# A hybrid decoder layer on one core: a third PSUM bank for the input projection, taken from the depthwise convolution's running sum

## The chip, the core and the metric

The kernel runs on one core of a Trainium2 chip. Five engines work side by side, each through its own queue in order: TensorE (PE in the profile, its weight loads PEld), VectorE (DVE), ScalarE (ACT), GpSimd (POOL) and SyncE (SP), which only issues transfers; ScalarE issues some too. They wait for each other by semaphores. SBUF is the working memory, PSUM holds matmul results in banks of 128 x 512 fp32 values. The metric is the device time of one launch in microseconds; less is better.

## What is computed

One layer over 2048 tokens of width 1024, all in fp32. A normalized input is projected once to 3080 columns, which feed three mixers; their outputs are joined, projected and added, and a SwiGLU feed-forward of inner width 2816 follows.

```python
h = rms_norm(x, norm1_g[l])
u = jnp.einsum('btd,de->bte', h, w_in[l])
u_conv, u_qkv, u_z, u_ab, u_dq, u_dk, u_dv = jnp.split(u, [...], axis=-1)
y_conv = conformer_conv_mixer(u_conv, ...)      # gate, 31-tap depthwise conv, layer norm, silu
y_gdn = gated_deltanet_mixer(u_qkv, u_z, u_ab, ...)   # chunks of 64, triangular solve, scan
y_diff = differential_attention_mixer(u_dq, u_dk, u_dv, ...)  # causal, two softmaxes per head
y = jnp.concatenate([y_conv, y_gdn, y_diff], axis=-1)
x = x + jnp.einsum('bte,ed->btd', y, w_out[l])
h = rms_norm(x, norm2_g[l])
gate, up = jnp.split(jnp.einsum('btd,df->btf', h, w_ffn_in[l]), 2, axis=-1)
x = x + jnp.einsum('btf,fd->btd', jax.nn.silu(gate) * up, w_ffn_out[l])
return rms_norm(x, final_norm_g)
```

The convolution: for each of 256 channels and each token, the sum over 31 earlier values of `val * sigmoid(gate)` times a weight, plus a bias.

## The kernel before

Tokens are worked in four units of 512 (`U`). Every large product is done three times in a two-part format: weights and activations are split into a high and a low part, and `mm3` (lines 136 to 139) adds high x high, high x low and low x high into one bank. A weight piece comes from memory as `wr`; ScalarE writes its high part (line 120) and GpSimd the low part as a difference (line 121), in two halves each, into one of three buffers `wp`. For the input projection the split pieces are also written to memory (`ws`, line 124), so units 1 to 3 load them without a split. Thus the splits of the input projection, and their GpSimd work, lie in unit 0 alone.

The steps of the first part are named in the string at line 937, two characters each, kind and unit: I is the projection to `mz` (gate columns) and `mq` (six tiles of q, k, v for the delta net, each with a 4-tap convolution, lines 321 to 336), C the projection to `mg` and `mv` and the 31-tap convolution, K the attention's q and k (`ma`, eight tiles), V its values (`mw`), N the input norm (`ht`), L the layer norm after the convolution, and G the delta net: products `kk`, the solve of 62 short VectorE operations in series (lines 466 to 472, `tm` and `Tt`, ended by the copy to `Lg` at line 473), a way through memory (`gT`, back to `X64`), the products `yp` and `wp`, and a scan over chunks (`vp`, `op`, `dp`). A0 is the attention of unit 0 (`s` scores, `pt` transposes, `po` output).

A projection tile takes its bank from `mmt` in turn (line 181: two banks, `mm0` and `mm1`). It is free when ScalarE and VectorE have taken the result out: for `ma` and `mw` ScalarE writes the high part (`qh`, `ve`), then VectorE the low part (`ql` at lines 708 and 711, `ve` at 728), and both go to memory from two buffers.

The convolution (`conv_taps`, lines 583 to 594) runs on VectorE. Per unit and per tile of 128 channels it does 31 operations of 512 columns: the first multiplies and adds the bias (line 591), thirty multiply and add (line 593). The sum stands in one PSUM bank `cp` (pool `ps_ca`, line 190), and the last operation writes it to SBUF, `ca`. As there is one bank, the second channel tile begins when the first is done.

At A0 the pool context `p1bctx` closes (line 955) and its four banks become those of the attention (`b0`, lines 956 to 958): scores, transposes, and outputs.

The order within each engine's queue is not written by hand. A scheduler with its own time estimates places every instruction; `hp(n)` raises the priority of what is inside it. So a change of pools or operations moves instructions on all engines, also where the diff touches nothing. After the first part, attention of units 1 to 3 is interleaved with the output projection and feed-forward of earlier units.

Of the kernel before, what the change touches and what calls it, by code (L numbers as in the profile page):

```python
# [10 lines left out]
F32 = mybir.dt.float32  # L11
F32R = mybir.dt.float32r
AF = mybir.ActivationFunctionType
ALU = mybir.AluOpType
AX = mybir.AxisListType
PSUM = bass.MemoryType.PSUM
DRAM = bass.MemoryType.DRAM

P = 128
# [3 lines left out]
U = 512  # L23
# [24 lines left out]
def body(ctx: ExitStack, tc: tile.TileContext, x, norm1_g, w_in, conv_dw_w, conv_dw_b,  # L48
# [3 lines left out]
    V, G, A, T = nc.vector, nc.gpsimd, nc.scalar, nc.tensor  # L52
# [20 lines left out]
    def cst(shape, name):  # L73
        return const.tile(shape, F32, name=name, tag=name)
# [26 lines left out]
    def hp(n=4000):  # L101
        return tc.high_priority(offset=n)
# [54 lines left out]
    def slots(pool, tag, n):  # L157
        return [(pool, f"{tag}{i}") for i in range(n)]

    def bank(*b):  # L160
        return Rot([P, 512], F32, *b)
# [19 lines left out]
    mmt = bank(*slots(ps_mm, "mm", 2))  # L181
# [5 lines left out]
    p1bctx = ExitStack()  # L187
    ps_tp = p1bctx.enter_context(tc.tile_pool(name="ps_tp", bufs=2, space=PSUM))
    ps_ga = p1bctx.enter_context(tc.tile_pool(name="ps_ga", bufs=1, space=PSUM))
    ps_ca = p1bctx.enter_context(tc.tile_pool(name="ps_ca", bufs=1, space=PSUM))  # L190


    x0 = [p1b.tile([P, D], F32, name=f"x1_0_{tt}", tag=f"x1{tt}") for tt in range(2)]
# [20 lines left out]
    cwT = cst([P, 2, 34], "cwT")  # L214
# [368 lines left out]
    def conv_taps(u, hc):  # L583

        acc2 = gd.tile([P, 2, U], F32, name=f"ca{u}", tag="ca")
        for ct in range(2):
            acc = ps_ca.tile([P, U], F32, name=f"cp{u}_{ct}", tag="cp")
            for j in range(31):
                w, hj = cwT[:, ct, j:j + 1], hc[:, ct, j:j + U]
                if j == 0:  # L590
                    V.tensor_scalar(acc, hj, w, cwT[:, ct, 31:32], op0=ALU.mult, op1=ALU.add)
                else:
                    V.scalar_tensor_tensor(acc2[:, ct, :] if j == 30 else acc, hj, w, acc, op0=ALU.mult, op1=ALU.add)  # L593
        return acc2

    def conv_ln(u, acc2):
# [81 lines left out]
    def conv_in(u):  # L678

        hts = HT[u]  # L680
        hc = gd.tile([P, 2, 30 + U], F32, name=f"hc{u}", tag="hc")
        G.tensor_copy(hc[:, :, 0:30], hist30)
        for ct in range(2):
            pg = mmt(f"mg{u}_{ct}")
            x_tile8(pg, hts, w_col_piece(w_in, COL_CONV + 256 + ct * P))
            tg_ = hc[:, ct, 30:30 + U]
            with hp():
                A.activation(tg_, pg, AF.Tanh, scale=0.5)
            pv = mmt(f"mv{u}_{ct}")
            x_tile8(pv, hts, w_col_piece(w_in, COL_CONV + ct * P))  # L690
            with hp():
                V.scalar_tensor_tensor(hc[:, ct, 30:30 + U], tg_, 1.0, pv, op0=ALU.add, op1=ALU.mult)
        G.tensor_copy(hist30, hc[:, :, U:U + 30])
        return hc
# [229 lines left out]
    def cut(t, n, m):  # L924

        return [t[:, i * n:(i + 1) * n] for i in range(m)]
# [10 lines left out]
    for step in ("I0 C0 G0 V0 N1 K0 L0 I1 G1 N2 C1 L1 K1 V1 I2 G2 C2 N3 K2 I3 G3 L2 C3 V2 A0 K3 V3 L3").split():  # L937
        what, u = step[0], int(step[1])
        if what == "N":
            HT[u] = ln1(u)  # L940
        elif what == "I":
            gdn_in(u)
        elif what == "G":
            with hp(GP):
                gdn_unit(u, QT[u], SC[u])
        elif what == "K":
            attn_qk(u)
        elif what == "V":
            attn_v(u)
        elif what == "C":  # L950
            CV[u] = conv_taps(u, conv_in(u))
        elif what == "L":
            conv_ln(u, CV[u])
        else:
            p1bctx.close()
            ps0 = ctx.enter_context(tc.tile_pool(name="ps0", bufs=1, space=PSUM, reuse_waits="tile"))
            b0 = slots(ps0, "b0", 4)
            sct, ptt, tot, pot = (bank(b) for b in b0)
            E0, W0 = (p1b.tile([P, 4096], F32, name=f"arena{g}", tag=f"ht{g}") for g in range(2))
            X0, X1 = (p1b.tile([P, D], F32, name=f"arenx{g}", tag=f"x1{g}") for g in range(2))  # L960
            Ep, Wp = cut(E0, 1024, 4), cut(W0, 1024, 4)
            Eq = [e[:, 512:1024] for e in Ep]
            AT.update(e0=Views(F32, *(e[:, 0:512] for e in Ep)), dm=Views(F32, Eq[0]), ob=Views(F32, *cut(Eq[1], 256, 2)),
                      e1=Views(F32, *Eq[2:4]), on=Views(F32, *(f3(c_) for c_ in cut(X0[:, 0:512], 256, 2))),
                      vv=Views(F32R, f4(Wp[0])), kk=Views(F32R, *cut(Wp[1], 512, 2)), pp=Views(F32R, f3(Wp[2])),
                      qq=Views(F32R, *(f3(c_) for c_ in cut(Wp[3], 512, 2) + cut(X1, 512, 2))))
            so_ = [0]

            def take(w, m):
                o = so_[0]  # L970
                so_[0] += w * m
                vs_ = cut(X0[:, 512 + o:], w, m)
                return Views(F32, *([v.rearrange("p (a b) -> p a b", a=2) for v in vs_] if w == 4 else vs_))
            AT.update(small(take))
            dm = dists(U)
            run(attn_unit(0))
# [287 lines left out]
```

## Time and profile before

| what | value |
|---|---|
| median of 3 runs | 2919.01 us (2917.42 to 2922.89) |
| profiled execution | 2917.14 us |
| its span | 2915.4 us |
| TensorE busy | 2800.1 us, 96% |
| VectorE busy | 1565.9 us, 54% |
| ScalarE busy | 1050.0 us, 36% |
| GpSimd busy | 1111.3 us, 38% |
| mean granted TensorE clock | 0.982 |

Durations come from the profiled execution. Shares over the whole span mix stages with different limits, so the tables by stretch count for more. Of a wait the trace names the instruction that came last. Names in the trace leave out the numbers of buffers: `ql` stands for all such tiles. [...]

### The profile page before, as it was taken

The numbers are of one execution on the slowest core, as the hardware profiler recorded it, in microseconds if no ns is written. First come the engines' busy times: TensorE is split into PE (matmuls) and PEld (weight loads), VectorE is DVE, ScalarE is ACT, GpSimd is POOL, SyncE is SP. The second block draws the span as 40 slices with busy tenths as digits, with TensorE's granted clock in tenths as the row PEclk, the third lists the DMA queues.
The fourth block names the chain that finished last, engine by engine and source line by source line (L and its number), as shares of the span: only waits on it lengthen the run. The fifth ranks groups of instructions, "written<-read, shape, count | busy, mean of one in ns | idle before, by whom it ended". The sixth has DMA issues, their size and how long they took to land.

```text
span 2915.4 us, 39754 instructions
## 1 busy us (share of the span) xinstructions
PE 2800.1 (96%) x14673; PEld 2284.4 (78%) x14673; DVE 1565.9 (54%) x3443; ACT 1050.0 (36%) x2237; POOL 1111.3 (38%) x1021
## 2 busy tenths in 40 slices
PE   7979989999988999999998999999999999999998
PEld 6867777778776788887877888887878888888886
DVE  8976776877766765565566655541332222422223
ACT  4333223322154544444455434442332222322222
POOL 4421010001033444344455434444644444444543
PEclk9989999999988999999999999999999999999999
DMA  7784573654776544444366344324343333323332
GB/s 253 242 274 153 178 232 127 207 179 138 254 200 219 144 131 122 112 126 118 108 182 203 86 130 120 93 88 151 102 149 99 96 94 101 116 87 102 101 94 87
DMA packets 404064, 422.52 MB, mean 145 GB/s; under 512 B 46448, under 2 KB 326170, under 8 KB 392606
## 3 DMA queue, kind: packets, MB, share of 16 engines
q1 hardware_dynamic: 344222, 373.31, 41.8%
q10 hardware_dynamic: 59648, 46.67, 5.1%
q8 instruction: 116, 1.90, 0.3%
q14 instruction: 78, 0.64, 0.1%
HBM read 344.35 MB, written 75.56 MB: 144 GB/s over the span
## 4 chain that ended last, share of the span: by engine, by line
PE 80%; DVE 8%; DMA 6%; issue 2%; ACT 2%; POOL 1%; ACTq 0%; SPq 0%; POOLq 0%; DVEq 0%
PE pg L137 6%; PE pg L138 6%; PE pg L139 6%; PE pu L139 5%; PE pu L137 5%; PE pu L138 5%; PE pd L137 5%; PE pd L138 5%; PE pd L139 5%; PE s L784 3%; PE pt L830 2%; PE po L137 1%; PE po L138 1%; PE po L139 1%; PE ma L137 1%
## 5 line engine op out<-in xcount | busy, mean ns | idle before, releaser
L121 POOL TENSOR_TENSOR wp<-wr,wp 128x512 fp32r<-128x512 f32 (+1 forms) x666 | 906.7, 1386 | 865.4 <-ACT wp L120 847.9
L120 ACT CAST wp<-wr 128x512 fp32r<-128x512 f32 (+1 forms) x666 | 378.6, 617 | 871.5 <-PE pd L139 229.1
L137 PE MATMUL pd<-wp,ac 128*128 128x512 f32 x704 | 279.8, 400 | 9.2 <-DVE x L1154 7.6
L1154 DVE TENSOR_TENSOR x<-x,pd 128x512 f32<-128x512 f32 x192 | 130.4, 685 | 285.6 <-PE pd L139 285.2
L137 PE MATMUL pg<-h,wp 128*128 128x512 f32 x704 | 279.6, 397 | 3.4 <-ACT h L1075 1.7
L138 PE MATMUL pd<-wp,ac 128*128 128x512 f32 x704 | 277.1, 394 | 2.1 <-POOL wp L121 2.1
L139 PE MATMUL pd<-wp,ac 128*128 128x512 f32 x704 | 277.5, 394 | 1.5 <-DVE ac L1138 1.5
L139 PE MATMUL pu<-h,wp 128*128 128x512 f32 x704 | 278.4, 396 | 0.0
L139 PE MATMUL pg<-h,wp 128*128 128x512 f32 x704 | 278.3, 395 | 0.0
L137 PE MATMUL pu<-h,wp 128*128 128x512 f32 x704 | 277.3, 394 | 0.6 <-DVE ft L1135 0.6
L138 PE MATMUL pu<-h,wp 128*128 128x512 f32 x704 | 277.8, 395 | 0.0
L138 PE MATMUL pg<-h,wp 128*128 128x512 f32 x704 | 277.6, 394 | 0.0
L1134 DVE SCALAR_TENSOR_TENSOR ft<-ft,pg 128x512 f32<-128x512 f32 x88 | 60.4, 686 | 244.1 <-ACT ft L1133 244.1
L784 PE MATMUL s<-kk,qq 128*128 128x512 f32 (+3 forms) x576 | 171.6, 384 | 5.5 <-DVE mx L787 5.1
L593 DVE SCALAR_TENSOR_TENSOR cp<-hc,cwT,cp 128x512 f32<-128x512 f32 x232 | 173.2, 747 | 2.5
L137 PEld LDWEIGHTS pd<-wp,ac 128*128 128x128 f32 x704 | 132.7, 188 | 45.8 <-DVE x L1154 15.1
L137 PEld LDWEIGHTS pg<-h,wp 128*128 128x128 f32 x704 | 132.3, 188 | 36.2 <-ACT wp L120 5.4
L139 PEld LDWEIGHTS pd<-wp,ac 128*128 128x128 f32 x704 | 132.5, 188 | 31.7 <-DVE ac L1138 3.1
L138 PEld LDWEIGHTS pd<-wp,ac 128*128 128x128 f32 x704 | 132.8, 189 | 30.2 <-POOL wp L121 3.5
L137 PEld LDWEIGHTS pu<-h,wp 128*128 128x128 f32 x704 | 132.3, 188 | 30.0 <-ACT wp L120 1.0
L138 PEld LDWEIGHTS pu<-h,wp 128*128 128x128 f32 x704 | 132.3, 188 | 29.7
L138 PEld LDWEIGHTS pg<-h,wp 128*128 128x128 f32 x704 | 132.3, 188 | 28.8 <-DVE h L1076 0.2
(389 smaller groups left out, 5866.0 us busy)
## 6 DMA issues: line engine op xcount, KB each, us to landing
wr<-in_w_ffn_in_dram SPq DMA_DIRECT2D x176, 512.0 KB, 3.9
wp<-ws SPq DMA_DIRECT2D x66, 1024.0 KB, 5.8
wr<-in_w_ffn_out_dram SPq DMA_DIRECT2D x88, 512.0 KB, 3.5
ws<-wp SPq DMA_DIRECT2D x22, 1024.0 KB, 6.9
wr<-in_w_out_dram SPq DMA_DIRECT2D x44, 512.0 KB, 3.6
arena<-vs SPq DMA_DIRECT2D x80, 256.0 KB, 3.8
kk<-ks SPq DMA_DIRECT2D x64, 256.0 KB, 5.0
qq<-qs SPq DMA_DIRECT2D x96, 128.0 KB, 4.5
```

The costliest lines, as they stand in the source:

```text
L120: A.copy(w[:, 0, q], raw[:, q])
L121: G.tensor_tensor(w[:, 1, q], raw[:, q], w[:, 0, q].bitcast(F32), op=ALU.subtract)
L137: T.matmul(ps, lhsT=lh, rhs=rh, start=start, stop=False)
L138: T.matmul(ps, lhsT=lh, rhs=rl, start=False, stop=False)
L139: T.matmul(ps, lhsT=ll, rhs=rh, start=False, stop=stop)
L593: V.scalar_tensor_tensor(acc2[:, ct, :] if j == 30 else acc, hj, w, acc, op0=ALU.mult, op1=ALU.add)
L784: T.matmul(sp[:, 0:w], lhsT=qq[c][:, l, q0:q0 + P], rhs=kt_[x][c][:, k0:k0 + w], start=l == 0, stop=l == 1)
L830: T.transpose(pt[:, col:col + P], ptile[b][kt // 8][:, (kt % 8) * P:(kt % 8 + 1) * P], ident)
L1134: V.scalar_tensor_tensor(t_, t_, 1.0, pg, op0=ALU.add, op1=ALU.mult)
L1154: V.tensor_tensor(xs_, xs_, pd, op=ALU.add)
```

## The change

The convolution's sum moves from the PSUM bank `cp` to the SBUF tile `ca`, where its result was written anyway; all 31 operations of a channel tile now read and write there. The bank goes to a pool `ps_m3`, which is added to the rotation of `mmt` as a third bank up to A0. There it is taken out again, as the attention uses all four banks.

```diff
     ps_tp = p1bctx.enter_context(tc.tile_pool(name="ps_tp", bufs=2, space=PSUM))
     ps_ga = p1bctx.enter_context(tc.tile_pool(name="ps_ga", bufs=1, space=PSUM))
-    ps_ca = p1bctx.enter_context(tc.tile_pool(name="ps_ca", bufs=1, space=PSUM))
+    ps_m3 = p1bctx.enter_context(tc.tile_pool(name="ps_m3", bufs=1, space=PSUM))
+    mmt.add((ps_m3, "mm2"))
...
         for ct in range(2):
-            acc = ps_ca.tile([P, U], F32, name=f"cp{u}_{ct}", tag="cp")
+            a = acc2[:, ct, :]
             for j in range(31):
                 w, hj = cwT[:, ct, j:j + 1], hc[:, ct, j:j + U]
                 if j == 0:
-                    V.tensor_scalar(acc, hj, w, cwT[:, ct, 31:32], op0=ALU.mult, op1=ALU.add)
+                    V.tensor_scalar(a, hj, w, cwT[:, ct, 31:32], op0=ALU.mult, op1=ALU.add)
                 else:
-                    V.scalar_tensor_tensor(acc2[:, ct, :] if j == 30 else acc, hj, w, acc, op0=ALU.mult, op1=ALU.add)
+                    V.scalar_tensor_tensor(a, hj, w, a, op0=ALU.mult, op1=ALU.add)
...
             p1bctx.close()
+            mmt.slots.pop()
```

Every engine has the same instructions as before, apart from the operands of the taps. Their order changes. In the changed kernel the lines stand one further down from line 190 on.

VectorE, where the solve of unit 0 begins, before. `cp0_1` is the sum of the second channel tile, `ql0_1544_0` the low part of the first q tile, `tm0_0` and `Tt0` the first step of the solve, `ht1` the activations of unit 1.

```order
L593 SCALAR_TENSOR_TENSOR cp0_1_1026<-hc0_850,cwT_126,cp0_1_1026 128x512 x2
L711 SCALAR_TENSOR_TENSOR ql0_1544_0_2086<-ma0_1544_0_2051,qh0_1544_0_2085 128x512
L593 SCALAR_TENSOR_TENSOR cp0_1_1026<-hc0_850,cwT_126,cp0_1_1026 128x512
L470 TENSOR_TENSOR tm0_0_1157<-Lg0_1151,Tt0_1152 64x31
L303 SCALAR_TENSOR_TENSOR ht1_1_1914<-ntp1_1_1_1970,g1T_118,ht1_1_1914 128x128
L303 SCALAR_TENSOR_TENSOR ht1_0_1913<-ntp1_2_0_1991,g1T_118,ht1_0_1913 128x128
```

The same place in the changed kernel; `ca0` is the sum of both channel tiles.

```order
L594 SCALAR_TENSOR_TENSOR ca0_993<-hc0_850,cwT_126,ca0_993 128x512
L304 SCALAR_TENSOR_TENSOR ht1_1_1912<-ntp1_1_1_1968,g1T_118,ht1_1_1912 128x128
L712 SCALAR_TENSOR_TENSOR ql0_1544_1_2124<-ma0_1544_1_2089,qh0_1544_1_2123 128x512
L304 SCALAR_TENSOR_TENSOR ht1_0_1911<-ntp1_1_0_1955,g1T_118,ht1_0_1911 128x128
L304 SCALAR_TENSOR_TENSOR ht1_1_1912<-ntp1_1_1_1968,g1T_118,ht1_1_1912 128x128 x2
L471 TENSOR_TENSOR tm0_0_1155<-Lg0_1149,Tt0_1150 64x31
L473 TENSOR_TENSOR Tt0_1150<-Tt0_1150,tm0_0_1155 64x31
L471 TENSOR_TENSOR tm0_1_1158<-Lg0_1149,Tt0_1150 64x60
```

All 62 taps of unit 0 now stand ahead of the solve (47 of them ahead of the last `kk` eviction); before it was 50 ahead of the solve (35 ahead of that eviction) and 12 between its steps.

TensorE, where the first products of the delta net's unit 0 (`yp0`) stand, before. `mz1_0` and `mz1_1` are tiles of unit 1's projection, `ctq` and `ctp` transposes of the layer norm.

```order
L139 MATMUL mz1_0_2454<-wp26_2449,ht1_1_1914 128x264
L616 MATMUL ctq0_1_2400<-ident_74,cxn0_1_2398 128x128
L604 MATMUL ctp0_2_2405<-ident_74,ca0_993 128x128 x2
L490 MATMUL yp0_1260<-X64_157,L0_477 32x32 x16
L137 MATMUL mz1_1_2484<-wp25_2447,ht1_0_1913 128x264
```

And in the changed kernel.

```order
L138 MATMUL mz1_0_2452<-wp26_2447,ht1_1_1912 128x264
L491 MATMUL yp0_1258<-X64_157,L0_477 32x32 x32
L617 MATMUL ctq0_0_2381<-ident_74,cxn0_0_2379 128x128
L617 MATMUL ctq0_1_2398<-ident_74,cxn0_1_2396 128x128
L139 MATMUL mz1_0_2452<-wp26_2447,ht1_1_1912 128x264
```

`yp0` moved forward, from behind 18 matmuls of `mz1_0` to behind 14, and stands in one piece.

TensorE, where the last unit's `yp3` stands, before. `s0_2_0_0` is a score tile of attention head 0, `mw3_0_2` a value tile of unit 3.

```order
L138 MATMUL mw3_0_2_8608<-wp97_8551,ht3_1_5714 128x256
L490 MATMUL yp3_6818<-X64_157,L3_6285 32x32 x32
L784 MATMUL s0_2_0_0_7777<-arena1_7698,arenx1_7700 128x384 x2
L139 MATMUL mw3_0_2_8608<-wp97_8551,ht3_1_5714 128x256
L137 MATMUL mw3_0_2_8608<-wp97_8551,ht3_1_5714 128x256
```

And in the changed kernel, where the last `mw3` matmul stands further up; `s2` and `po1` belong to heads 2 and 1.

```order
L831 MATMUL pt1_1_0_7945<-ident_74,arena0_7689 128x128 x3
L605 MATMUL ctp3_2_8803<-ident_74,ca3_7392 128x128 x2
L785 MATMUL s2_2_0_0_8059<-arena1_7690,arenx1_7692 128x384 x2
L491 MATMUL yp3_6812<-X64_157,L3_6279 32x32 x16
L605 MATMUL ctp3_3_8820<-ident_74,ca3_7392 128x128 x2
L844 MATMUL po1_1_7944<-arena1_7690 128x256
```

The attention's first score `s0_0` moved forward, from among the `mw3_0_0` matmuls to among those of `ma3_1544_2`, and `yp3` moved back behind all projection tiles.

## Rows read from the trace of the kernel before

**Rows 1.** The page's head and its first part: span, and busy time, share and instructions of each engine.

```profile
span 2915.4 us, 39754 instructions
PE 2800.1 (96%) x14673; PEld 2284.4 (78%) x14673; DVE 1565.9 (54%) x3443; ACT 1050.0 (36%) x2237; POOL 1111.3 (38%) x1021
```

**Rows 2.** The table by stretches: from and to, length, busy time of each engine with its instructions, granted clock, DMA share, GB/s.

```profile
100.00:213.00 113.00, 95.10 (x555) 80.17 (x554) 94.95 (x208) 37.10 (x88) 32.79 (x29) 0.91 0.80 270
213.00:395.00 182.00, 180.47 (x1195) 141.73 (x1194) 134.65 (x329) 55.43 (x133) 18.26 (x20) 0.99 0.54 178
395.00:445.00 50.00, 39.23 (x273) 35.50 (x272) 29.94 (x106) 11.89 (x31) 5.26 (x7) 0.88 0.65 205
445.00:640.00 195.00, 192.53 (x1222) 151.83 (x1220) 154.56 (x381) 56.57 (x132) 16.93 (x16) 1.00 0.57 181
640.00:800.00 160.00, 157.78 (x1100) 127.64 (x1101) 118.75 (x283) 37.54 (x79) 17.22 (x19) 0.98 0.57 185
```

**Rows 3.** Whom TensorE waits for in the first 1000 us: total, times, longest, in us.

```profile
PE ma L137 <- DVE ql L711: 13.7, 3, 8.2
...
PE yp L490 <- DMA X<-gT: 4.7, 3, 2.4
...
PE mw L137 <- DVE ve L728: 2.4, 1, 2.4
```

**Rows 4.** Three instructions around the longest of these waits, from the order of time on ScalarE, VectorE and TensorE: start, duration, engine, line, operation, out<-in, and in brackets the idle time before and what ended it.

```profile
160.64 0.59 ACT L710 ACTIVATE qh<-ma 128x512 fp32r<-128x512 f32 x1
...
168.86 0.67 DVE L711 SCALAR_TENSOR_TENSOR ql<-ma,qh 128x512 fp32r<-128x512 f32 x1
...
169.68 0.77 PE L137 MATMUL ma<-ht,wp 128*128 128x512 f32 x1 [8.19 <-DVE ql L711]
```

**Rows 5.** The table by stretches for the first unit up to the end of its solve; the third busy time is VectorE's.

```profile
100.00:199.00 99.00, 83.53 (x492) 70.72 (x491) 89.98 (x198) 33.21 (x77) 32.24 (x28) 0.90 0.77 262
```

**Rows 6.** The way from the solve of unit 0 to `yp`: the last `kk` eviction, the transfer that brings the matrix back (from the chain of waits: start and duration), the first step of the solve, the copy that ends it, the transfers back, and `yp` on TensorE.

```profile
137.38 0.28 DVE L456 TENSOR_TENSOR Q<-kk,Q 128x128 f32<-128x128 f32 x1
...
143.13 12.86 DMA Lg<-gL
...
156.08 0.20 DVE L470 TENSOR_TENSOR tm<-Lg,Tt 64x31 f32<-64x31 f32 x1 [0.23 <-DMA Lg<-gL]
...
199.15 1.12 DVE L473 COPY Lg<-Tt 64x1024 f32<-64x1024 f32 x1
...
205.93 1.18 ACTq L480 DMA_DIRECT2D X<-gT  x2
...
212.85 1.19 PE L490 MATMUL yp<-X,L 32*32 32x32 f32 x32
```

**Rows 7.** The taps, and the same operations of the 4-tap convolution with all operands in SBUF (lines 330 and 328): shortest, median and longest duration in ns, first and last start in us.

```profile
L593 DVE SCALAR_TENSOR_TENSOR cp<-hc,cwT,cp x232: 721/746/757, 101.5 to 784.8; 128x512 f32<-128x512 f32 x116
...
L591 DVE TENSOR_SCALAR cp<-hc,cwT x8: 802/808/814, 100.7 to 739.8; 128x512 f32<-128x512 f32 x8
...
L330 DVE SCALAR_TENSOR_TENSOR cc<-ut,qwT,cc x72: 734/752/1852, 47.5 to 656.0; 128x512 f32<-128x512 f32 x72
...
L328 DVE TENSOR_SCALAR cc<-ut,qwT x24: 469/480/1592, 46.0 to 652.1; 128x512 f32<-128x512 f32 x24
```

**Rows 8.** Two pairs of weight splits on GpSimd and the 4-tap convolution beside them, in order of time (neighbours of one form are merged, with their count).

```profile
45.89 2.76 POOL L121 TENSOR_TENSOR wp<-wr,wp 128x512 fp32r<-128x512 f32 x2 [1.86 <-PE gcs L370]
...
45.99 1.50 DVE L328 TENSOR_SCALAR cc<-ut,qwT 128x512 f32<-128x512 f32 x1
...
47.53 3.24 DVE L330 SCALAR_TENSOR_TENSOR cc<-ut,qwT,cc 128x512 f32<-128x512 f32 x3
...
55.26 3.93 POOL L121 TENSOR_TENSOR wp<-wr,wp 128x512 fp32r<-128x512 f32 x2 [6.62 <-ACT wp L120]
...
56.26 1.78 DVE L330 SCALAR_TENSOR_TENSOR cc<-ut,qwT,cc 128x512 f32<-128x512 f32 x1
```

**Rows 9.** A pair of splits and the 31-tap convolution beside it.

```profile
104.03 2.81 POOL L121 TENSOR_TENSOR wp<-wr,wp 128x512 fp32r<-128x512 f32 x2 [3.08 <-ACT wp L120]
...
104.38 4.71 DVE L593 SCALAR_TENSOR_TENSOR cp<-hc,cwT,cp 128x512 f32<-128x512 f32 x6
```

**Rows 10.** GpSimd in the stretches from the first to the last tap of each unit: length, busy time and instructions, clock, DMA share, GB/s. The first row counts the splits (line 121) alone, the others all of GpSimd, for units 1, 2 and 3.

```profile
100.70:171.20 70.50, 23.54 (x18) 0.94 0.85 284
...
298.20:390.00 91.80, 7.47 (x9) 1.00 0.66 210
500.40:588.00 87.60, 6.66 (x8) 1.00 0.64 191
670.10:786.30 116.20, 11.59 (x14) 1.00 0.63 207
```

**Rows 11.** The last unit: `yp` of unit 3, the last matmul of the value projection, the first of the feed-forward, and two stretches between them.

```profile
801.34 1.17 PE L490 MATMUL yp<-X,L 32*32 32x32 f32 x32 [0.77 <-DMA X<-gT]
...
833.61 0.28 PE L139 MATMUL mw<-wp,ht 128*128 128x256 f32 x1
...
992.17 0.50 PE L137 MATMUL pg<-h,wp 128*128 128x512 f32 x1 [0.47 <-DVE h L1076]
...
834.00:992.00 158.00, 142.39 (x800) 111.24 (x799) 117.72 (x349) 79.95 (x213) 66.96 (x80) 0.88 0.71 201
```

## The prediction

> **What bounds the kernel now.** I read the page first, then the table of stretches, then who TensorE waits for, then single lines. The profiled execution took 2917.1 us for a span of 2915.4 us [rows 1]; the rest, 1.7 us, lies around the span. The median of the runs is 2919.0 us, 1.9 us above the profiled one. I sum against 2917.1 and add 1.9 at the end.
>
> TensorE is busy for 96% of the span [rows 1], so a change here can save little, but it can cost anything. By stretches [rows 2] the picture is uneven. From 213 us on TensorE is the bound: 180.5 of 182 us, and again 192.5 of 195 and 157.8 of 160. Two stretches before the attention are different. From 100 to 213 us TensorE is busy for only 95.1 of 113 us at a granted clock of 0.91, and VectorE for 95.0. From 395 to 445 us TensorE loses 10.8 us.
>
> What TensorE waits for is what the change is about [rows 3]: 13.7 us in three waits of the q/k projection (`ma`) for VectorE's `ql`, and 2.4 us in one wait of the v projection (`mw`) for `ve`. These are waits for a bank: with two banks a third tile cannot begin before the first is evicted. 16.1 us is all that the third bank can save directly.
>
> The three `ma` waits lie at 155 to 182 us, inside the first unit. Take the largest [rows 4]: ScalarE had written `qh` at 160.64, but VectorE came to `ql` only at 168.86, and TensorE went on at 169.68. VectorE was not idle: from 100 to 199 us it worked for 90.0 of 99.0 us [rows 5]. It is the bound of the first unit, with the 62 convolution taps of that unit, the transposed activations of unit 1 (`ht`) and the serial triangular solve (`tm`, `Tt`) in one queue.
>
> **How VectorE's queue reaches TensorE there.** The last eviction of the `kk` products ends at 137.7 us, the matrix goes out and comes back, and the solve begins at 156.08, the moment its data land. It ends with the copy at 199.15; that is written out, read back by transfers issued from 205.93 on, and TensorE's `yp`, which reads them, starts at 212.85 [rows 6]. So `yp` stands 13.7 us behind the end of the solve, and whatever delays the solve delays everything that TensorE's queue holds behind `yp`.
>
> **The taps.** Each is one multiply-add of 512 columns, 31 per channel tile, 62 per unit, 248 in all. Now: 746 ns, never over 757 (and 808 for the first of a tile) [rows 7]. The nearest row for the new form, all operands in SBUF, is the short convolution: the same operation and size, median 752, but up to 1852 [rows 7]. Median against median the taps cost the same; the 8 first taps go from 808 to about 480 ns by the row of the short convolution's first, which saves 0.7 us in unit 0.
>
> What makes 1852 is GpSimd. A pair of weight splits runs at 45.89; the first multiply beside it takes 1.50 instead of 0.48, and the three that follow take 3.24 instead of 2.26. A second pair at 55.26 holds one multiply for 1.78, and is itself stretched from 2.76 to 3.93 [rows 8]. So each split that meets such an operation costs VectorE about 1.0 us. The present taps don't notice: six in a row take 4.71 us beside a pair of splits [rows 9].
>
> How many splits lie beside the taps of unit 0? 18, with 23.5 us, from 100.7 to 171.2 us [rows 10]. At 1.0 us that is 18 us if each holds a tap; none if all fall beside operations that read PSUM. Taps are most of what VectorE does in that stretch, so I take 15. VectorE's own idle time there, 9.0 us of 99.0, can take up some; I take 4, because most of it is waiting for operands that come later too. 15 - 4 - 0.7 = 10.3 us on the end of the solve, bounds 0 and 18.
>
> [...]
>
> In the order of VectorE the cover is gone too: 47 taps stand ahead of the last `kk` eviction instead of 35, and none is left beside the solve, where 12 stood. The solve starts later and runs tighter; its end moves only by what is added in total.
>
> **TensorE in the first unit.** The bank waits of 13.7 us go, in part. But then TensorE only comes to `yp` earlier, and waits there. In its new order `yp` stands after 14 of the first `mz1` matmuls instead of after 18, so 4 of them, about 0.5 us, are left for afterwards. Term: +10.3 + 0.5 = +10.8 us. The gain of the bank in this unit is therefore nothing, except where the solve is not what ends last.
>
> **Units 1 and 2.** Beside their taps GpSimd has 9 and 8 short operations, 7.5 and 6.7 us, and no splits [rows 10]; VectorE is busy for 134.7 of 182 us and 154.6 of 195 [rows 2], and TensorE has work, so the few holds are hidden. The wait of 2.4 us for `ve` may go. Against it, TensorE already waited for the solve's data at `yp` in later units, 4.7 us in three waits [rows 3], and this can grow by as much. Bounds -2.4 and +4.7; I take 0.
>
> **Unit 3 and the start of attention.** The convolution no longer owns a bank that attention needs. In the order the first score `s0_0` moves from beside `mw3_0_0` up to beside `ma3_1544_2`, and `yp3`, the start of the last scan, moves from beside `mw3_0_2` to behind all `mw3`, beside head 2. Now `mw3` ends at 833.6, `yp3` starts at 801.34 and the feed-forward at 992.17 [rows 11]. From 834 to 992 TensorE is busy for 142.4 of 158 us at a clock of 0.88 [rows 11]: 15.6 us idle, and 0.12 x 158 = 19 us of clock.
> The upper bound: the chain from `yp3` to the feed-forward, 190.8 us, keeps its length and begins at 834 instead of 801, so 33 us late; but in those 33 us attention work is done that stood elsewhere (two heads move ahead, under projection matmuls), of which I count half: +17. The lower bound: with two heads under projections the idle 15.6 us vanish: -16. Neither is nearer to a row, so I take +2. The taps of unit 3 stand beside 14 GpSimd operations, 11.6 us [rows 10], and VectorE is busy for 118.8 of 160 us [rows 2], which hides them.
>
> **Sum.** 2917.1 + 10.8 + 0 + 2 = 2929.9; plus 1.9 for the median: 2932 us.
>
> **Rivals.**
> 1. The third bank is what counts: VectorE's holds fall into its 9.0 us of idle time and beside PSUM operations, the bank waits go. For it: 13.7 us of real waiting for evictions. Against it: VectorE's 91% in that stretch, and the `yp` chain. 2919.0 - 16.1 = 2903 us. Decides for it: fewer than about 9 of 18 splits hold a tap.
> 2. Unit 0 as forecast, but the earlier start of attention pays in full: +10.8 - 16, so 2914; with half of that 2921. This is the case of no change.
> 3. Unit 0 as forecast, and the last scan, which now runs without projections beside it, delays the feed-forward by its bound: +10.8 + 17 + up to 4.7 for waits at `yp`: 2947 to 2952.
> 4. The taps themselves become shorter in SBUF. The only row for it is the first tap (808 against 480 ns): 0.33 x 62 = 20 us less on VectorE in unit 0, more than the holds add. Then 15 - 20 gives no delay, and the bank saves perhaps half of its 16: 2911. Against it: 752 against 746 for the very operation.
> [...]
>
> **How the numbers follow.** About 0.2%, 5.8 us, is what can be told from no change: 2913.2 to 2924.8. Forecast, slower by some 13 us (2922 to 2942): 0.50. Rival 3 (2942 to 2955): 0.14. Rival 2 (2911 to 2924): 0.18. Rival 1 (2898 to 2911): 0.13. Rival 4 (2905 to 2915): 0.05. Faster: rival 1 whole, most of rival 4 and a little of rival 2, 0.18. Same: the rest of rival 2 and the lowest part of the forecast, 0.20. Slower: 0.62. The range leaves out the lower third of rival 1 and a part of rival 3, and reaches from 2906 to 2951; the forecast's own is 2922 to 2942.
>
> **What would show it.** In the profile after: the taps with a median near 750 ns but a maximum of 1.7 to 1.9 us; their mean higher in unit 0 alone; the copy that ends the first solve near 210 us instead of 199; a wait of TensorE at the first `yp` of 10 us or more for the transfer that it reads; no wait of `ma` for `ql` over 3 us. I am wrong if taps stay under 760 ns throughout, if the first `yp` still starts by 213 us, or if the feed-forward starts before 992 us.

## The result, and the profile after

The changed kernel takes 2962.8 us (median of 4 runs, 2960.4 to 2969.8); the kernel before took 2920.5 in the same comparison. The ratio is 1.015, interval 1.0135 to 1.0165: slower by 42 us, where 13 were forecast and 2951 was the upper end of the range.

The page's head and first part, after (before: [rows 1]).

```profile
span 2961.4 us, 39696 instructions
PE 2827.4 (95%) x14673; PEld 2303.5 (78%) x14673; DVE 1573.9 (53%) x3443; ACT 1049.0 (35%) x2237; POOL 1120.8 (38%) x1021
```

The span is 46 us longer. The next two views say where. First the table by stretches of the kernel after: from and to, length, busy time of each engine with its instructions, granted clock, DMA share, GB/s. The first five answer to [rows 2].

```profile
100.00:213.00 113.00, 95.73 (x518) 79.95 (x519) 105.88 (x199) 33.71 (x77) 38.33 (x29) 0.88 0.76 253
213.00:395.00 182.00, 179.18 (x1157) 139.39 (x1156) 133.93 (x326) 58.22 (x139) 20.51 (x21) 0.98 0.56 178
395.00:445.00 50.00, 42.75 (x335) 40.28 (x334) 33.37 (x110) 11.73 (x29) 5.05 (x7) 0.93 0.75 238
445.00:640.00 195.00, 192.12 (x1250) 151.85 (x1248) 152.42 (x383) 56.80 (x135) 16.43 (x16) 0.99 0.56 178
640.00:800.00 160.00, 159.73 (x1072) 128.33 (x1072) 106.28 (x273) 41.62 (x91) 20.40 (x22) 0.99 0.59 191
786.00:838.00 52.00, 43.18 (x300) 37.79 (x298) 49.87 (x120) 17.67 (x49) 22.58 (x20) 0.87 0.69 215
786.00:1050.00 264.00, 226.69 (x1340) 181.20 (x1339) 182.22 (x497) 107.02 (x277) 90.93 (x102) 0.79 0.58 167
```

The same two last stretches of the kernel before:

```profile
786.00:838.00 52.00, 48.11 (x468) 43.96 (x468) 26.37 (x88) 22.40 (x58) 17.03 (x20) 0.93 0.67 197
786.00:1050.00 264.00, 244.34 (x1527) 200.87 (x1527) 177.87 (x514) 126.88 (x319) 101.93 (x122) 0.92 0.65 183
```

Up to 800 us nothing of size is lost: TensorE runs 4332 matmuls in the first five stretches, 4345 before. From 786 to 838 VectorE, the third busy time, goes from 26.4 to 49.9 of 52 us and TensorE falls from 48.1 to 43.2. From 786 to 1050 TensorE is idle for 37.3 us instead of 19.7, and the granted clock, a share of full, is 0.79 instead of 0.92: (1 - 0.79) x 264 = 55 us of clock instead of 21. They overlap in part: from 840 to 860 us TensorE was busy for 15.4 of 20 us, and was granted 0.50, half clock. Their growth, 34 and 18 us, adds up to about the 51 us by which the feed-forward starts later.

The last unit line by line, after (before: [rows 11]): first attention score, last value projection, last tap, end of the last solve, first `yp` of the unit, first matmul of the feed-forward.

```profile
747.39 0.34 PE L785 MATMUL s<-arena 128*128 128x128 f32 x2
...
821.13 0.28 PE L139 MATMUL mw<-wp,ht 128*128 128x256 f32 x1
...
832.57 2.30 DVE L594 SCALAR_TENSOR_TENSOR ca<-hc,cwT,ca 128x512 f32<-128x512 f32 x1
...
837.19 1.03 DVE L474 COPY Lg<-Tt 64x1024 f32<-64x1024 f32 x1
...
848.21 1.91 PE L491 MATMUL yp<-X,L 32*32 32x32 f32 x32 [2.53 <-DMA X<-gT]
...
1043.50 0.48 PE L137 MATMUL pg<-h,wp 128*128 128x512 f32 x1
```

`yp` starts 46.9 us later than in [rows 11], the feed-forward 51.3 us; from the one to the other it is 195.3 us, 190.8 before. The last tap stands at 832.6; in [rows 7] the last that writes `cp` stands at 784.8.

The taps, and the way through unit 0, after (before: [rows 6, 7 and 9]): shortest, median, longest in ns; then single lines, a pair of splits, the tap beside it, the copy that ends the solve, and the two groups of `yp`.

```profile
L594 DVE SCALAR_TENSOR_TENSOR ca<-hc,cwT,ca x240: 724/744/2301, 102.5 to 832.6; 128x512 f32<-128x512 f32 x120
L592 DVE TENSOR_SCALAR ca<-hc,cwT x8: 533/542/551, 101.9 to 746.0; 128x512 f32<-128x512 f32 x8
```

```profile
104.51 3.15 POOL L121 TENSOR_TENSOR wp<-wr,wp 128x512 fp32r<-128x512 f32 x2 [2.34 <-ACT wp L120]
...
106.45 1.77 DVE L594 SCALAR_TENSOR_TENSOR ca<-hc,cwT,ca 128x512 f32<-128x512 f32 x1
...
209.47 1.10 DVE L474 COPY Lg<-Tt 64x1024 f32<-64x1024 f32 x1
...
217.91 1.19 PE L491 MATMUL yp<-X,L 32*32 32x32 f32 x32
...
221.43 1.91 PE L491 MATMUL yp<-X,L 32*32 32x32 f32 x32 [2.33 <-DMA X<-gT]
```

Two of TensorE's waits in the first 1000 us, after (before: [rows 3]; the three for `ql` lie in unit 0 again):

```profile
PE yp L491 <- DMA X<-gT: 14.8, 5, 6.1
PE ma L137 <- DVE ql L712: 10.2, 3, 4.4
```

On VectorE unit 0 came as forecast. The copy that ends its solve moved from 199.15 to 209.47, by 10.3 us. Of its 62 taps 14 lasted over 1 us, each beside a split, and all 62 sum to 59.3 us instead of 46.5. On TensorE it did not: the first `yp` starts 5.1 us later and without a wait, where a wait of 10 us or more was the sign, and of the 13.7 us of bank waits 10.2 remain.

### The profile page after: what moved, and what is told of

It is laid out like the page before. It is cut to its first block, busy times and chain, and to the rows that moved or that the text cites. A ratio compares the mean times of both kernels' runs of the same rounds, so it can differ in the third digit from the quotient of the medians.

```text
span 2961.4 us, 39696 instructions
## 1 busy us (share of the span) xinstructions
PE 2827.4 (95%) x14673; PEld 2303.5 (78%) x14673; DVE 1573.9 (53%) x3443; ACT 1049.0 (35%) x2237; POOL 1120.8 (38%) x1021
## 4 chain that ended last, share of the span: by engine, by line
PE 81%; DVE 9%; DMA 4%; issue 2%; POOL 1%; ACT 1%; SPq 1%; ACTq 0%; POOLq 0%; DVEq 0%
PE pg L137 6%; PE pg L138 5%; PE pg L139 5%; PE pu L139 5%; PE pu L138 5%; PE pu L137 5%; PE pd L137 5%; PE pd L138 5%; PE pd L139 5%; PE s L785 3%; DVE ca L594 2%; PE pt L831 2%; PE ma L137 2%; PE ma L138 2%; PE ma L139 2%
## 5 line engine op out<-in xcount | busy, mean ns | idle before, releaser
L594 DVE SCALAR_TENSOR_TENSOR ca<-hc,cwT,ca 128x512 f32<-128x512 f32 x240 | 192.3, 820 | 1.2
L137 PEld LDWEIGHTS pd<-wp,ac 128*128 128x128 f32 x704 | 132.2, 188 | 43.9 <-DVE x L1156 15.8
L138 PEld LDWEIGHTS pu<-h,wp 128*128 128x128 f32 x704 | 132.3, 188 | 30.0
L139 PEld LDWEIGHTS pd<-wp,ac 128*128 128x128 f32 x704 | 132.2, 188 | 29.9 <-DVE ac L1140 1.2
L139 PEld LDWEIGHTS pu<-h,wp 128*128 128x128 f32 x704 | 132.3, 188 | 29.0 <-POOL wp L121 0.4
L137 PEld LDWEIGHTS pu<-h,wp 128*128 128x128 f32 x704 | 132.3, 188 | 28.9
```

Of the source, the lines that this page charges most:

```text
L137: T.matmul(ps, lhsT=lh, rhs=rh, start=start, stop=False)
L138: T.matmul(ps, lhsT=lh, rhs=rl, start=False, stop=False)
L139: T.matmul(ps, lhsT=ll, rhs=rh, start=False, stop=stop)
L594: V.scalar_tensor_tensor(a, hj, w, a, op0=ALU.mult, op1=ALU.add)
```

## The experiments

Each was timed beside the kernel before on the same chip; the medians of the kernel before were 2917.9 to 2921.3 us. In the table, the ratio is to those runs; "clock" is (1 - granted clock) x 264 us from 786 to 1050 us, "idle" is TensorE's in the same stretch, "FF" the first feed-forward matmul, all of the profiled execution.

| kernel | us | ratio (95%) | FF | clock | idle |
|---|---|---|---|---|---|
| before | 2920 | 1 | 992 | 21 | 20 |
| changed | 2962.8 | 1.0135 to 1.0165 | 1044 | 55 | 37 |
| changed_again | 2972.0 | 1.0162 to 1.0196 | 1048 | 50 | 38 |
| u0_only | 2933.5 | 1.0033 to 1.0069 | 1000 | 18 | 24 |
| u3_only | 2938.4 | 1.0027 to 1.0069 | 1047 | 26 | 36 |
| u3_psum | 2927.4 | 1.0002 to 1.0040 | 1009 | 26 | 27 |
| no_bank | 2943.1 | 1.0045 to 1.0096 | 1036 | 29 | 34 |
| mid_bank | 2924.8 | 1.0006 to 1.0026 | 1006 | 29 | 26 |
| a0_late | 2939.1 | 1.0040 to 1.0082 | 1016 | 29 | 30 |
| bank_out | 2950.3 | 1.0077 to 1.0161 | 1037 | 32 | 31 |
| bank_u3 | 2952.3 | 1.0093 to 1.0139 | 1051 | 34 | 40 |
| fill_po | 2949.9 | 1.0088 to 1.0131 | 1043 | 18 | 31 |
| before_fill10 | 2914.0 | 0.9958 to 0.9987 | 998 | 16 | 14 |
| before_fill5 | 2934.0 | 1.0022 to 1.0057 | 1009 | 21 | 23 |
| late_fill10 | 2944.2 | 1.0053 to 1.0108 | 1014 | 16 | 23 |
| mid_fill10 | 2925.9 | 0.9998 to 1.0027 | 991 | 8 | 20 |
| wait_only | 2934.3 | 1.0047 to 1.0080 | 1006 | 21 | 28 |
| raw_sum | 2906.9 | 0.9952 to 0.9982 | 988 | 13 | 16 |
| l2_early | 2903.5 | 0.9944 to 0.9984 | 990 | 16 | 23 |
| raw_mid | 2906.7 | 0.9949 to 0.9979 | 995 | 13 | 29 |

**First group: which part?** Theory A blamed the attention's earlier place in the order, B GpSimd's holds on the taps, C the third bank. The four kernels pick the units whose taps are in SBUF and the steps in which the bank takes part.

u3_only (bank pool as before, no third bank):

```diff
-            acc = ps_ca.tile([P, U], F32, name=f"cp{u}_{ct}", tag="cp")
+            a = ps_m3.tile([P, U], F32, name=f"cp{u}_{ct}", tag="mm2") if u in (0, 1, 2) else acc2[:, ct, :]
```

> The kernel before, with the taps of unit 3 alone summed in SBUF; units 0 to 2 keep the PSUM bank, and there is no third bank. Theory A (the order in unit 3: attention no longer waits for the convolution's bank, is placed ahead of the last taps and of the last solve, and the last scan then runs without projections beside it at half clock): nearly the whole loss, 2952 to 2966 us, the feed-forward some 45 to 55 us later than 992, mean granted clock about 0.97. Theory B (VectorE is held by GpSimd in taps whose operands are all in SBUF): only the 14 GpSimd operations beside the taps of unit 3, so 2920 to 2928. Theory C (the third bank reorders TensorE): 2920, as there is none.

It cost 18 us, half of what A asked and far more than B or C allow. The feed-forward came at 1046.5 as A said, but the part behind it took 1891 us instead of 1923, as attention work had been done ahead of it (6003 matmuls ahead of the feed-forward, 5838 before).

u3_psum (the changed kernel but for unit 3; the bank leaves the rotation ahead of its taps):

```diff
-            a = acc2[:, ct, :]
+            a = ps_m3.tile([P, U], F32, name=f"cp{u}_{ct}", tag="mm2") if u in (3,) else acc2[:, ct, :]
...
+            if u == 3:
+                mmt.slots.pop()
...
```

> The changed kernel, with the taps of unit 3 alone back in a PSUM bank: the third bank leaves the rotation before them and holds their sum. Theory A: the loss goes but for what unit 0 costs (its solve ends 10 us late, of which the units behind it had regained 8), 2918 to 2930, feed-forward near 992 to 1002. Theory B: the holds of unit 0 stay, so at least 10 of the 42 us, and those of units 1 and 2; 2945 to 2960. Theory C: 2955 to 2963, the bank is there through units 0 to 2.

2927 us, in A's range, though the feed-forward came at 1009, 7 us later than A allowed. So units 0 to 2 hold some 7 us of the loss (1 to 12 by the interval), and unit 3 the rest. B and C fall as main causes.

a0_late:

```diff
-    for step in ("... I3 G3 L2 C3 V2 A0 K3 V3 L3").split():
+    for step in ("... I3 G3 L2 C3 V2 K3 A0 V3 L3").split():
```

> The changed kernel, taps in SBUF throughout and the third bank as it is; only the step of the first attention stands one place later in the list of steps, behind the attention's q and k of unit 3 (K3), so the scheduler ranks it lower. Theory A: the order in unit 3 comes back, taps and solve end some 40 to 50 us earlier than in the changed kernel, 2918 to 2935 us, mean granted clock 0.98. Theory B: 2955 to 2965, since every tap is held as before. Theory C: 2950 to 2965.

Faster than the changed kernel by 24 us or more, but above A's range, and for the wrong reason: the attention now started late (803.9), and still the last tap stood at 823.1, not 40 us earlier. So the attention had not pushed the taps back. That is what A had claimed, and this run speaks against it.

no_bank (all taps in SBUF, `mmt.add` left out):

> All taps in SBUF, but the freed bank is left empty and the projections keep two. Theory A: as the changed kernel, 2955 to 2970, with the bank waits of the q and k projection back (up to 16 us, hidden at least in part). Theory B: the same 2955 to 2970. Theory C: 2918 to 2930.

2943: no theory's range. The bank was worth 8 us on the first solve (its end was 217.9 without, 209.5 with), and yet the kernel with it was slower.

**Second group: the clock.** changed_again is the changed kernel unaltered, in company of the others.

> The changed kernel once more, beside the other variants of this group on one chip. If the half-clock stretches of 61 and 31 us around 824 and 937 us belong to the kernel's order of work: 2955 to 2968 us, mean granted clock 0.967 to 0.972, and the same stretches at half clock. If they were an accident of that execution: 2935 to 2945 us at 0.976 to 0.979, as the variants with the same late last scan (taps of unit 3 alone in SBUF: 2938; without the third bank: 2943).

2972, 4 us above the range, and a clock of 0.81 in the stretch: it belongs to the kernel. Then fill_po, which adds unused work to it:

```diff
+            if HALF == U:
+                for f in range(10):
+                    T.matmul(po[:, 256:512], lhsT=vt[0][:, 0, 0, :], rhs=vt[0][:, 0, 0:2, :].rearrange("p t c -> p (t c)"),
+                             start=g == 0 and f == 0, stop=False, skip_group_check=True)
```

> The changed kernel with 120 matmuls more, which compute nothing that is used: ten of 128x256 ahead of each output group of the first attention, into the unused half of its bank, where TensorE would wait for the transposed scores to be evicted. By the value projection's 192 matmuls in 31 us they are about 19 us of TensorE work at full clock, some 11 of it between 820 and 970 us. Theory A (the granted clock is what costs, and it falls because TensorE waits there): the clock lost before the feed-forward falls from 84 us to under 65, and the time does not grow, 2935 to 2965. Theory D (the chain of scan, attention and VectorE sets the time, and the low clock only goes with it): the clock may rise, but the time stays or grows by the added work, 2963 to 2985, and the feed-forward still begins at 1043 or later.

With 120 matmuls more it was 22 us faster than changed_again. TensorE's clock from 786 to 1050 and one operation of the last scan in both kernels show how; first the changed kernel (the stretch of changed_again, then two lines of the first profile at either clock, and two stretches of 20 us):

```profile
786.00:1050.00 264.00, 225.88 (x1343) 179.57 (x1342) 186.70 (x508) 108.52 (x279) 92.33 (x102) 0.81 0.60 171
```

```profile
931.66 0.67 PE L543 MATMUL vp<-kd,X 64*64 64x64 f32 x8
...
937.68 1.11 PE L543 MATMUL vp<-kd,X 64*64 64x64 f32 x8
...
920.00:940.00 20.00, 17.31 (x120) 13.11 (x119) 9.92 (x22) 5.67 (x17) 8.18 (x8) 0.93 0.52 165
940.00:960.00 20.00, 20.00 (x86) 14.15 (x86) 10.59 (x37) 5.97 (x14) 1.39 (x3) 0.50 0.14 34
```

and fill_po:

```profile
786.00:1050.00 264.00, 233.36 (x1548) 190.83 (x1547) 194.62 (x550) 118.42 (x300) 92.17 (x107) 0.93 0.65 182
...
944.04 0.68 PE L543 MATMUL vp<-kd,X 64*64 64x64 f32 x8
...
940.00:960.00 20.00, 19.20 (x140) 14.02 (x137) 17.73 (x63) 11.75 (x24) 6.31 (x8) 1.00 0.61 161
```

The clock lost in the stretch fell from 50 to 18 us, and half clock is a cost of its own here: the eight matmuls shown took 1.11 us at it, and 0.67 or 0.68 at full clock. But the 22 us are not the clock's alone, as the order moved too: ahead of the shown operation, from 927 to 939 us, fill_po has 36 matmuls of 512 columns (`hp`). Of the gain 6 us lie ahead of the feed-forward (1042.5 instead of 1048.4) and 15 behind it, where less work was left. Nor is half clock the root. In other kernels the same filler paid for itself at best (mid_fill10, before_fill10) or not at all:

> The kernel before with five unused matmuls of 128x256 ahead of each output group of the first attention, 60 in all, about 10 us of TensorE work at full clock. In the kernel before 22 us of clock are lost between 786 us and the feed-forward. Theory A: at least a third of it comes back and pays for the added work, 2908 to 2922 us. Theory D (waits set the time): 2920 to 2930.

> The kernel before with ten unused matmuls ahead of each output group, 120 in all, about 19 us of TensorE work at full clock. Theory A: half of the 22 us of clock comes back, but the work added is as much or more, 2912 to 2930 us. Theory D: 2925 to 2940.

> The changed kernel with the first attention one place later in the list of steps (2939 us without a filler, 29.0 us of clock lost between 786 us and the feed-forward) and the ten unused matmuls per output group. Theory A: the clock lost falls under 20 us, 2920 to 2938 us. Theory D: 2940 to 2958.

> Third bank and taps in SBUF for units 1 and 2 alone (2925 us without a filler, 29.0 us of clock lost between 786 us and the feed-forward), with the ten unused matmuls per output group. Theory A: the clock lost falls under 20 us, 2910 to 2926 us. Theory D: 2926 to 2944.

Ten per group gained 6 us in the kernel before, as A allowed; five lost 14, outside either range. The filler also moves the order, so 6 to 14 us either way may come from that; it was not separated. late_fill10 won 13 us of clock and 7 of idle time against a0_late, added 19 us of work (estimate: 120 matmuls at the 31 us of the value projection's 192) and was 5 us slower, in D's range; mid_fill10 won 21 of clock and was no faster than mid_bank, on the border of A and D.

u0_only and mid_bank completed the first group (the same condition in the tile line, with units 1 to 3, and with units 0 and 3, in PSUM; in mid_bank `mmt.add` at step I1 and `pop` ahead of unit 3's taps).

> The kernel before with the taps of unit 0 alone summed in SBUF; units 1 to 3 in PSUM, no third bank. Theory A: the end of the first solve is some 10 us late (205 to 215 instead of 199), most of it is regained in units 1 and 2, and unit 3 is as before: 2920 to 2932 us. Theory B (the holds of VectorE by GpSimd are the main loss): 2945 to 2960.

> Taps of units 0 and 3 in the PSUM bank, those of units 1 and 2 in SBUF; the bank joins the projections' rotation from unit 1's projection on and leaves it ahead of unit 3's taps. Theory A: unit 0 and the start of attention as before, and the 2.4 us wait for ve goes, perhaps some of the 10.8 us that TensorE loses from 395 to 445: 2910 to 2922. Theory C (a third bank reorders TensorE to its harm): 2925 or more.

Without the third bank the holds of unit 0 (its longest tap took 1.78 us) put the end of the first solve at 218.9, 19.7 us late instead of 10.3 and later than expected, and cost 14 us, just over A's range. mid_bank was no gain: 2925, between the two ranges.

**Third group: the bank in unit 3.** bank_out pops it at step I3, bank_u3 adds it there to u3_only.

> The changed kernel, all taps in SBUF, but the third bank leaves the projections' rotation at unit 3's input projection, so unit 3 runs on two. Theory E (the third bank in unit 3 makes TensorE finish the projections earlier while the last taps and solve stay where they are, which deepens the half clock): as without the bank, 2935 to 2948 us, last mw3 matmul at 826 us or later, under 35 us of clock lost between 786 us and the feed-forward. Theory F (it is a matter of how the instructions happen to fall once the last scan is late, not of the bank in unit 3): no such pattern, 2950 to 2975 as likely as 2940.

> The kernel before with units 0 to 2 as they were (taps in the PSUM bank, two banks for projections); the bank joins the rotation at unit 3's input projection and unit 3's taps are summed in SBUF. Theory E: like the changed kernel in unit 3, so well over the 2938 us of unit 3's taps in SBUF alone: 2955 to 2970 us, over 45 us of clock lost between 786 us and the feed-forward. Theory F: near 2938 us, 2930 to 2948.

Both lie between 2938 and 2963 to 2972, and neither theory's pattern came out whole. In bank_out single runs reach from 2944 to 2968: the loss behind a late last scan is not a fixed price.

**Fourth group: why are the taps late?** What the slow kernels with the sum of unit 3 in `ca` share is seen when the first tap of unit 3 is put beside the last instruction that reads `ca` of unit 2, the end of that unit's layer norm (`cy`, line 624). After:

```profile
744.60 0.69 DVE L624 SCALAR_TENSOR_TENSOR cy<-cy,ca 128x512 f32<-128x512 f32 x1 [0.88 <-ACT cy L623]
745.54 0.99 DVE L592 TENSOR_SCALAR ca<-hc,cwT 128x512 f32<-128x512 f32 x2
```

u3_only:

```profile
734.72 0.67 DVE L623 SCALAR_TENSOR_TENSOR cy<-cy,ca 128x512 f32<-128x512 f32 x1
735.95 0.98 DVE L591 TENSOR_SCALAR ca<-hc,cwT 128x512 f32<-128x512 f32 x2
```

a0_late:

```profile
751.25 0.69 DVE L624 SCALAR_TENSOR_TENSOR cy<-cy,ca 128x512 f32<-128x512 f32 x1
752.19 0.99 DVE L592 TENSOR_SCALAR ca<-hc,cwT 128x512 f32<-128x512 f32 x2
```

In all nine profiles of such kernels, the changed one's two included, the first tap starts 0.9 to 2.1 us behind that read. The trace shows the wait as a place in VectorE's queue, not as idle time put down to `ca`. And before, where the first tap of unit 3 did not wait, but the 31st, which writes `ca`, did:

```profile
670.09 0.81 DVE L591 TENSOR_SCALAR cp<-hc,cwT 128x512 f32<-128x512 f32 x1
...
711.08 0.74 DVE L593 SCALAR_TENSOR_TENSOR cp<-hc,cwT,cp 128x512 f32<-128x512 f32 x1
...
737.89 0.68 DVE L623 SCALAR_TENSOR_TENSOR cy<-cy,ca 128x512 f32<-128x512 f32 x1
...
738.82 0.73 DVE L593 SCALAR_TENSOR_TENSOR ca<-hc,cwT,cp 128x512 f32<-128x512 f32 x1
```

`ca` has one buffer. In the kernel before a tile's sum stands in PSUM, so 30 taps run ahead of the wait. In the changed kernel the first tap already writes `ca`, and all 62 stand behind it: 32 of them after 786 us, where none was before. There they share VectorE with the last solve and the attention. (u0_only and before_fill5 are some 14 us slower without this wait.) This is theory G; four kernels test it. raw_sum:

```diff
-            a = acc2[:, ct, :]
+            a = acc2[:, ct, :] if u == 0 else wpool.tile([P, WS], F32, name=f"cp{u}_{ct}", tag="wraw", bufs=2)[:, :U]
...
-                    V.scalar_tensor_tensor(a, hj, w, a, op0=ALU.mult, op1=ALU.add)
+                    V.scalar_tensor_tensor(acc2[:, ct, :] if j == 30 else a, hj, w, a, op0=ALU.mult, op1=ALU.add)
```

> The changed kernel with its third bank, but from unit 1 on the running sum stands in a weight buffer that is idle then (wraw), and only the last tap writes ca. Theory G (with the sum in ca, the first tap of unit 3 waits until the layer norm of unit 2 has read ca for the last time: it starts at 745.5, 0.9 us behind that read at 744.6, instead of at 670; ca has one buffer): the first tap of unit 3 starts by 700, its solve ends by 815, the feed-forward starts by 1012, and the time is 2918 to 2935 us. Theory F (how the instructions fall): 2940 to 2970.

l2_early:

```diff
-    for step in ("... C2 N3 K2 I3 G3 L2 C3 V2 A0 K3 V3 L3").split():
+    for step in ("... C2 N3 K2 L2 I3 G3 C3 V2 A0 K3 V3 L3").split():
```

> The changed kernel; only the layer norm of unit 2 (L2) stands two places earlier in the list of steps, ahead of unit 3's input projection, so ca is read and free sooner. Theory G: the first tap of unit 3 starts by 700, 2918 to 2938 us. Theory F: 2940 to 2970.

raw_mid (raw_sum, with unit 0 in the PSUM bank `mm2` and `mmt.add` at step I1):

> Unit 0's taps in the PSUM bank as before (no holds by GpSimd), the bank joins the projections' rotation at unit 1's projection and stays until the first attention; sums of units 1 to 3 in the idle weight buffer, as in raw_sum. Theory G: neither the unit 0 term nor the wait for ca is left, 2908 to 2924 us. Theory F: 2930 to 2960.

wait_only, on the kernel before:

```diff
+            bias = cwT[:, ct, 31:32]
+            if u == 3:
+                V.tensor_copy(acc2[:, ct, 0:1], bias)
+                bias = acc2[:, ct, 0:1]
...
-                    V.tensor_scalar(acc, hj, w, cwT[:, ct, 31:32], op0=ALU.mult, op1=ALU.add)
+                    V.tensor_scalar(acc, hj, w, bias, op0=ALU.mult, op1=ALU.add)
```

> The kernel before with taps in the PSUM bank and two projection banks; only the bias of unit 3's first taps is copied into ca and read from there, so that they wait for ca as in the changed kernel (the attention then waits for the late taps too, through their bank). Theory G: the first tap of unit 3 moves from 670 to 725 or later, its solve ends at 815 or later, and the time is 2932 to 2960 us, most of the loss of the changed kernel with nothing else of it. Theory F or A (the freed bank): 2916 to 2928.

All four went G's way. The first tap of unit 3 in raw_sum:

```profile
669.33 0.54 DVE L592 TENSOR_SCALAR cp<-hc,cwT 128x512 f32<-128x512 f32 x1
```

In l2_early it is free of the layer norm:

```profile
637.81 0.68 DVE L624 SCALAR_TENSOR_TENSOR cy<-cy,ca 128x512 f32<-128x512 f32 x1
664.98 0.54 DVE L592 TENSOR_SCALAR ca<-hc,cwT 128x512 f32<-128x512 f32 x1
...
793.98 1.12 DVE L474 COPY Lg<-Tt 64x1024 f32<-64x1024 f32 x1
...
989.80 0.39 PE L137 MATMUL pg<-h,wp 128*128 128x512 f32 x1
```

The three kernels without the wait take 2903 to 2907 us, faster than the changed kernel by 56 us or more and than the kernel before by 11 to 14; all three were faster than G's ranges, raw_mid by 1 us. l2_early differs from the changed kernel only in where the layer norm of unit 2 stands in the list; raw_sum and raw_mid also give each channel tile a scratch tile of its own, where the kernel before has one bank for both. So it is not shown that the gain over the kernel before is the bank's. wait_only, last read and first tap:

```profile
732.49 0.68 DVE L627 SCALAR_TENSOR_TENSOR cy<-cy,ca 128x512 f32<-128x512 f32 x1
...
734.07 0.80 DVE L595 TENSOR_SCALAR cp<-hc,cwT,ca 128x512 f32<-128x512 f32 x1
```

The wait alone, put into the kernel before, moved its first tap to 734 and cost 16 us, in G's range, though the last solve ended at 806 and not at 815 or later. It keeps the attention's bank tied to the taps, so it isn't the whole of the changed kernel's case. With the early attention it costs 18 us (u3_only), with the third bank in unit 3 as well 31 (bank_u3), in the changed kernel 42 to 53; what each step adds was not separated from the order that it moves.

Whether l2_early's order would also speed up the kernel before was not tried.

## Why the prediction was wrong

The direction and unit 0 were right; the time was 31 us too low, and the step that failed is the one on unit 3.

- **Taps and holds.** Median 744 against 746, maximum 1.79 us in unit 0 and 2.30 in unit 3. 14 held taps were counted in unit 0 where 15 were taken, at 0.98 us each, about the 1.0 of the rows; with first taps that are 0.5 us shorter in all, the taps took 12.8 us more. In the trace the pair of splits at 104.51 ends at 107.66, and the tap that began beside it at 106.45 ends 0.56 us after that. A hold of 0.98 us is less than the 1.31 us of a split (23.54 us in 18 [rows 10]); that tap began 0.52 us behind the start of the pair's second split at 105.93. In [rows 8] a multiply with one tensor operand was held, 1.50 us instead of 0.48. Nor was unit 0 alone in being held: four taps of unit 3 lasted over 1 us, each beside a GpSimd instruction, and its 62 took 49.5 us instead of 46.3.
- **End of the first solve.** +10.3 us forecast and measured. But the agreement is luck: without the third bank the same holds put it 19.7 us late (u0_only), so the bank gave 9 us back, which I had put at nothing. From 100 to 213 us TensorE was busy for 95.7 us with the bank and for 88.5 in u0_only.
- **Its effect at the end.** I carried +10.8 us through to the end, by a wait of TensorE at the first `yp`. That wait did not come. raw_sum and raw_mid differ in unit 0 alone (solve ends at 210.2 and 201.0) and take the same time, 2906.9 and 2906.7. With the third bank in units 1 and 2 the delay is regained. So this term was too large: 0 to 7 us.
- **Units 1 and 2.** Taken as 0, bounds -2.4 and +4.7. u3_psum has units 0 to 2 as changed and is 7 us slower than before, less than the 10.8 that I had put on unit 0 alone. So no loss of size came from them, though TensorE's waits at `yp` grew from 4.7 to 14.8 us over all units, more than the bound had.
- **Unit 3, the step that failed.** "The taps of unit 3 stand beside 14 GpSimd operations, 11.6 us [rows 10], and VectorE is busy for 118.8 of 160 us [rows 2], which hides them", and "Neither is nearer to a row, so I take +2". I asked what the taps would meet at the place where they stood, not whether they could still stand there. They could not: the destination of the first tap had become a buffer that another step was reading. The order after showed `yp3` behind the last `mw3`, and I took that for the scheduler's choice. The hint was in [rows 7]: the last of the first operations of a tile starts at 739.8, so unit 3's second tile began 70 us after its first at 670.1 [rows 10], though 31 taps take 23 us. Something already held the last tap of the first tile. With the late taps `yp3` began at 848.2, where the upper bound had 834, and the feed-forward was 51.3 us late, so nothing was regained ahead of it, where the bound counted half back. The term of +2 came out at some 35 us: 42 less the 7 of u3_psum.
- **Rival 3** named the mechanism behind it, a last scan without projections beside it, and priced it at 17 us. u3_only, 18 us, is close to that; in the changed kernel it was some 35. The bound counted TensorE's work at an unchanged clock.
- **Rivals 1 and 2** expected a gain from the bank and from the early attention. Without the wait the change takes 2903 to 2907 us, where rival 1 had 2903; but the bank waits that rival 1 counted on are still there in the changed kernel, 10.2 of 13.7 us, and which of the two gives the gain was not tested. The match in size shows neither.

What stays open is why the same late scan costs 18 us in u3_only and 42 to 53 in the changed kernel. The feed-forward starts about equally late in both, at 1046.5 and at 1043.5 to 1048.4. The difference is what TensorE had done by then: 6003 of its matmuls in u3_only and 5908 in the changed kernel, where it lost more to the granted clock (50 to 55 us against 26); the part behind takes 1891 us in the one and 1918 to 1919 in the other. bank_out and bank_u3 lie between; which instruction tips it was not found.

## What to carry to other kernels

When an accumulation moves from a scratch bank into the tile that takes its result, the wait for that tile moves from the last operation to the first (here from the 31st tap, at 738.8 us, to the first, at 745.5): look for the last reader of the tile's previous contents, and put the two side by side in the trace before costing anything else. A row in which the second of two equal pieces starts far later than the first takes can be such a wait, already there. And a delay that leaves TensorE with short, waiting work must be priced with the clock that such a stretch was granted (here 0.79 from 786 to 1050 us), not at full clock.

## What the runs showed of the hardware

- In the changed kernel a stretch without idle time was at half clock. From 920 to 940 us TensorE was idle for 2.7 us and granted 0.93. From 940 to 960 us it was busy for 20.00 of 20 us, on the scan's tiles of 64 and on scores, and was granted 0.50 throughout; eight 64x64 matmuls took 0.67 us at 931.66 and 1.11 at 937.68. In fill_po, where 36 matmuls of 512 columns stand from 927 to 939 us, such eight took 0.68 in the stretch from 940 to 960, at 1.00.
- With 120 unused matmuls the changed kernel took 2949.9 us, 22 less than without (changed_again, 2972.0). Their places moved the order as well, and in three other kernels the same ten per group gave -6, +1 and +5 us.
- The first operation of a tile (multiply and add, one tensor operand) took a median of 542 ns with its sum in SBUF, in the changed kernel, and 808 in PSUM, before [rows 7]; the multiply-add with two tensor operands took 744 and 746.
